# Rows gathered for a sparse expert layer: first picks in the query phase, 16 extra tokens, scores copied after all three products

## The chip, the cores and the metric

The kernel runs on one core of one Trainium2 chip. The metric is the device time of one execution, in microseconds (us). The profile is of one execution; its times count from the first instruction, and the time of that execution is a little longer than its span.

The engines are called by the profile's names: PE multiplies matrices (PEld is its weight load), DVE works on vectors, ACT applies functions and copies, POOL does vector work and issues the indexed transfers, SP issues most of the plain transfers. An engine works through its own instructions in order. A matmul on 32-bit floats shows as two records in the profile.

## The reference

One step of a decoder layer for 336 tokens: 256 prompt tokens, 64 sample tokens (8 sequences of 8) and 16 learned ones that only prepare state. A first part (a convolution branch, a state-space mixer, projections) ends in `x`. The change touches the second part, an expert layer for 320 tokens:

```python
q = (xb @ w_q).reshape(T, 8, 2, 128)              # 8 heads, 2 halves
s = einsum('thcd,hckd->thck', q, keys)            # 128 keys for each half
s1, i1 = top_k(s[:, :, 0], 16);  s2, i2 = top_k(s[:, :, 1], 16)
cand = s1[..., :, None] + s2[..., None, :]        # 256 sums a head
sc, f = top_k(cand, 16)                           # 16 picks a head, 128 a token
ids = i1[f // 16] * 128 + i2[f % 16]              # of 16384 experts
act = gelu(einsum('thkd,td->thk', U[ids], xb))
y = einsum('thk,thkd->td', softmax(sc) * act, V[ids])
```

The last step adds `y` to `x` and normalizes.

## The kernel before

**Two ways to the same sum.** For most of the 320 tokens the kernel multiplies with all 16384 experts and then zeroes what wasn't picked: the dense way, `ND` = 184 tokens. For 128 tokens (`NGAT`) and 8 extra ones (`NX`) it fetches only the picked rows of U and V, 8 KB each, by an indexed transfer.

**Dense blocks.** `u_block(b)`, for 128 blocks of 128 experts, multiplies a 512 KB block of U with the tokens `nd` (8 matmuls of 184 columns into PSUM, line 1429), and ACT writes the gelu to `S` (line 1431). `v_block(b)`, again 128 times, multiplies a 512 KB block of V with `S[b]` into the sum `va` (line 1531). Blocks come into a ring of 8 buffers (`eraw`, line 1412); even blocks are issued on SP, odd ones mostly on ACT. The first 8 blocks of U lie in buffers of their own (`pre`) and are read ahead in the query phase. Between blocks `g_step` builds, for 8 tokens at a time and each half of the experts, the weights of the picks (DVE makes one-hot tiles `oh`, PE multiplies them into `pg`, DVE multiplies `S` by that).

**Gathered rows.** A column `c` of `gid` holds, for each of the 128 tokens, the number of one picked expert. `gather(c)` fetches 128 rows of 8 KB (U and V side by side) into one of 5 buffers `wuv` (`UV`). `pick_dot` multiplies with the token (DVE, line 1317), ACT applies gelu and the softmax weight (lines 1319 and 1322), `pick_sum` adds the V half into `ygat` (DVE, line 1327), which frees the buffer. The 8 extra tokens are laid out 16 times over the partitions, so that their 128 picks take 8 columns of 128 rows; their sums go to `acce`, and `group_sum` adds them up. In all that makes `NCOL` = 136 columns.

**Pace.** `gather` makes the transfer wait for a matmul of the fifth-last block issued in the program so far (`LEAD` = 4). `ahead(n)` issues columns `n` to `n+3` (to `n+1` in the second half of the V blocks). `Feed` deals the tasks out among the blocks: `NU` = (42, 26, 35) says how many columns are paired with the U blocks up to 84, with the other U blocks, and with the first 64 V blocks; the rest follow among the last V blocks up to block 126. The U blocks up to 84 also carry the ranking of the dense tokens (`topk_tasks`) and of heads 4 to 7 of the gathered ones. Some buffers of that ranking are given up at block 84.

**Query phase.** For each of 16 halves of heads (`j`), `weight` fetches 512 KB of `w_q` and splits it into a high part `wh` (ACT) and a low part `wl` (POOL, in four pieces, line 253), `proj` does 24 matmuls (line 182), ACT copies the result to `qT`, and three products with the keys, one for each group of 128, 128 and 64 tokens, give the scores `psc` (line 1206). ACT copies each to `sco` or `sall` (line 1208), and for the gathered tokens `top16` ranks them on DVE. Inside the loop a product is followed by its copy and then by the next product into the same tile. After `j` = 7, `heads_tasks(0)` ranks the candidate sums of heads 0 to 3 and writes `gid`, and `ahead(0)` issues the first gathers.

A scheduler sets the order of each engine's instructions from the program's order, the dependencies and its own clock; the order shown below is what it gave.

Of the kernel before, what the change touches and what calls it, by code (L numbers as in the profile page):

```python
# [7 lines left out]
F32 = mybir.dt.float32  # L8
# [25 lines left out]
PH = 8  # L34
NK = 128
# [1 line left out]
NM = T - T2  # L37
SQ = T2 - NQ * TS
NGAT = 128
NX = 8  # L40
XQ = 128 // max(NX, 1)
ND = T2 - NGAT - NX
NPICK = 128
NCOL = NPICK + (NPICK // XQ if NX else 0)
XAT = 64
HG = 4
EXTRA = 5
LEAD = 4
GT = 8
# [6 lines left out]
AGAIN = 24  # L56
HB = 64
KTILES = ((0, NGAT), (128, 128), (256, 64))
NU = (42, 26, 35)
LM = (0.05, 0.05, 0.1, 0.5, 0.999)  # L60
LOW = 400
NW0 = 3
# [9 lines left out]
LATER = 8  # L72
# [92 lines left out]
def body(tc, ia, oa, stop=None):  # L165
    nc = tc.nc
    with ExitStack() as top:
# [125 lines left out]
        def misc(shape, name):  # L293
            return ps.tile(shape, F32, name=name, tag="misc", bufs=2)
# [764 lines left out]
        def top16(vals, idx, v, h, late=False):  # L1059
            L = v.shape[0]  # L1060
            i_ = nc.vector.max(vals[:L, h, 0:8], v)
            if late:
                tc.add_manual_dep(i_.ins, early[0], mybir.DependencyInfo(mybir.DependencyClass.NoSync,
                                                                         mybir.DependencyReason.DATA),
                                  reason="gathered tokens first")
            nc.vector.max_index(idx[:L, h, 0:8], vals[:L, h, 0:8], v)  # L1066
            nc.vector.match_replace(v, vals[:L, h, 0:8], v, -3.0e38)
            nc.vector.max(vals[:L, h, 8:16], v)
            nc.vector.max_index(idx[:L, h, 8:16], vals[:L, h, 8:16], v)
# [45 lines left out]

        early = []

        def heads_tasks(h0):
            hs_ = slice(h0, h0 + HG)
            cs = slice(16 * h0, 16 * (h0 + HG))  # L1120
            st = {}

            def cand():
                st["sf"] = table(128, HG, si[0][:, 2 * h0:2 * h0 + 2 * HG])
                st["c"], st["cf"] = candidates(128, HG, sv[0].rearrange("p (h c) k -> p h c k", c=2)[:, hs_])

            def pick(half):
                if half == 0:
                    st["ab"] = places(128, HG, ci0.rearrange("p h k -> p (h k)")[:, cs])
                    st["pk"] = kp.tile([128, 2, HG * 16], F32, name="pkh")  # L1130
                look(st["pk"][:, half], 128, HG, st["ab"][half], st["sf"], half, st["c"])

            def soft():
                idf = kp.tile([128, HG * 16], F32, name="idh")
                nc.vector.scalar_tensor_tensor(idf, st["pk"][:, 0], float(NK), st["pk"][:, 1], op0=OP.mult, op1=OP.add)
                early.append(nc.vector.tensor_copy(gid[:, cs], idf).ins.name)
                g_ = kp.tile([128, HG, 16], F32, name="gh")
                nc.vector.tensor_tensor(g_, cv0[:, hs_], cv0[:, hs_, 0:1].to_broadcast([128, HG, 16]), op=OP.subtract)
                if h0:
                    nc.scalar.activation(g_, g_, AF.Exp, scale=rsT[:, 0:1])  # L1140
                else:
                    act(g_, g_, AF.Exp, scale=rsT[:, 0:1])
                sm = kp.tile([128, HG], F32, name="smh")
                nc.vector.tensor_reduce(sm, g_, axis=AX.X, op=OP.add)
                nc.vector.reciprocal(sm, sm)
                nc.vector.tensor_tensor(ggw[:, cs].rearrange("p (h k) -> p h k", k=16), g_,
                                        sm[:, :, None].to_broadcast([128, HG, 16]), op=OP.mult)

            return ([(1.5, cand)] + [(1.3, lambda h=h: top16(cv0, ci0, st["cf"][:, h], h0 + h)) for h in range(HG)]
                    + [(2.5, lambda: pick(0)), (2.0, lambda: pick(1)), (1.0, soft)])  # L1150

# [41 lines left out]
        for j in range(16):  # L1193
# [6 lines left out]
            proj(p[:, :T2], w, rows(ah[:, :, :T2], al[:, :, :T2]))  # L1200
            qT = qTs[j % 3]
            nc.scalar.copy(qT[:, :T2], p[:, :T2])
            p = misc([128, 3, NK], "psc")
            for i, (t0, L) in enumerate(KTILES):
                n, up = 2 * heads_of[i], 64 * (j // (2 * heads_of[i]))
                nc.tensor.matmul(p[:, i], qT[:, t0 - up:t0 - up + 128], keys[:, j, :], start=True, stop=True)
                s_ = sall[i][:, j % n] if i else kp.tile([128, NK], F32, name="sco", bufs=9)
                scored = nc.scalar.copy(s_[up:up + L], p[up:up + L, i]).ins.name
                if i == 0:
                    top16(sv[i], si[i], s_[:L], j)  # L1210
# [4 lines left out]
            if j == EXTRA:  # L1215
                extra_tokens()
                xs.close()
            if j == 2 * HG - 1:
                for _, f_ in heads_tasks(0):
                    f_()  # L1220
            if j == 2 * HG - 1:
                ahead(0)
        xqs.close()
        parts = [(0, SA), (SA, SB), (SB, 128)]
        Sm = []
# [122 lines left out]
        def take(n):  # L1348
            t = ops[:n]
            del ops[:n]  # L1350
            return t

        def mixin(a_, b_):
# [3 lines left out]
                out += b_[q * nb // na:(q + 1) * nb // na]  # L1357
            return out

        t1, t2 = topk_tasks(1), topk_tasks(2)  # L1360
        bg = mixin(t1[:-1] + t2[:-5] + t1[-1:] + t2[-5:-1], take(NU[0] - 4 - LATER)) + take(4) + t2[-1:]
        bg += mixin(heads_tasks(HG), take(LATER))

        class Feed:
            def __init__(self, tasks, steps):
# [302 lines left out]
```

## Time and profile before

| | before |
|---|---|
| three runs | 1278.71, 1280.62, 1280.56 us |
| median | 1280.56 us |
| the profiled execution | 1278.62 us |
| its span | 1276.8 us |
| busy DVE / ACT / POOL | 961.7 / 520.4 / 595.6 us |
| moved by the DMA engines | 373.82 MB, of it 142.62 MB by the 136 gathers |
| granted TensorE clock | 0.995 on the mean |

The span falls in three parts: the layer's first part up to 520 us, the query phase up to about 600 us (its last scores reach ACT at 619 us), and the dense blocks with the gathers, up to 1266 us, with a tail of 11 us.

In a row of the timeline stand the start, the duration, the engine, the line of the kernel, the operation, the tile written and those read, the shape, and how many instructions are merged; in brackets stands how long the engine had been idle and what released it. In a row by stretches stand, for each engine, busy us and the number of instructions, then the granted clock, the share of time that the 16 DMA engines were busy, and what they moved in GB/s.

### The profile page before, as it was taken

To read this page: it belongs to the slowest core of one execution; us is meant where nothing else is said; L and a number is where in the kernel's file an instruction comes from. 1 tells how busy PE (TensorE), PEld (TensorE's weight loads), DVE (VectorE), ACT (ScalarE), POOL (GpSimd) and SP (SyncE) were. 2 spreads that over 40 slices of the span, in tenths; PEclk is the share of its full clock that TensorE was granted. 3 is DMA by queue.
4 is the path that set the end of the run, shared out by engine and by line. 5 is a ranking of instruction groups with operands and counts; after the bars stand their busy time and mean duration, and the time that the engine had idled before them with its cause. 6 is when DMAs were issued, how large, how long until landed. Compare 5 with 4: busy or idle time off the path is not lost.

```text
span 1276.8 us, 23637 instructions
## 1 busy us (share of the span) xinstructions
PE 1257.3 (98%) x8953; PEld 1214.0 (95%) x8953; DVE 961.7 (75%) x2121; ACT 520.4 (41%) x1308; POOL 595.6 (47%) x595
## 2 busy tenths in 40 slices
PE   9999999999999999999999999999999999999997
PEld 7989999999889999999999999999999999999997
DVE  6888889888977335549999978888888888545555
ACT  6778777887766444544232222222210111001102
POOL 2487777887795766975132232223322322122110
PEclk9899999999999999999999999999999999999999
DMA  6435454344434444765989999999999999999994
GB/s 248 166 130 194 158 190 169 140 175 170 145 126 149 149 150 149 255 243 210 372 321 422 421 420 420 420 420 420 420 421 420 420 421 419 397 421 420 419 421 158
DMA packets 85618, 373.82 MB, mean 293 GB/s; under 512 B 9585, under 2 KB 15089, under 8 KB 65921
## 3 DMA queue, kind: packets, MB, share of 16 engines
q1 hardware_dynamic: 48048, 166.87, 34.9%
q0 software_dynamic: 19584, 142.62, 26.9%
q10 hardware_dynamic: 17872, 62.84, 12.2%
q8 instruction: 70, 1.15, 0.4%
q14 instruction: 44, 0.35, 0.1%
HBM read 359.24 MB, written 13.05 MB: 292 GB/s over the span
## 4 chain that ended last, share of the span: by engine, by line
PE 81%; DVE 15%; DMA 2%; ACT 1%; issue 1%; POOL 1%; ACTq 0%; DVEq 0%
PE pj L182 32%; PE va L1531 25%; PE pj L1429 15%; DVE wuv L1317 2%; DVE ygat L1327 2%; PE pg L1457 2%; DVE pcv L525 1%; PE pst L182 1%; DMA wuv<-in_peer_uv_dram,gid 1%; PE po L182 1%; PE py L182 1%; PE pq L182 1%; DMA wdt<-in_w_dt_dram 1%; DVE st L718 1%; DVE si L1066 1%
## 5 line engine op out<-in xcount | busy, mean ns | idle before, releaser
L1159 POOL DMA_INDIRECT wuv<-in_peer_uv_dram,gid x136 | 166.2, 1222 | 478.3 <-PE va L1531 133.7
L253 POOL TENSOR_TENSOR wl<-wraw,wh 128x256 fp32r<-128x256 f32 (+1 forms) x202 | 289.9, 1455 | 109.5 <-ACT wh L249 64.9
L1531 PE MATMUL va<-S,eraw 128*128 128x184 f32 x2048 | 325.4, 320 | 0.0
L1531 PEld LDWEIGHTS va<-S,eraw 128*128 128x128 f32 x2048 | 318.9, 190 | 0.9 <-issue 0.9
L1429 PE MATMUL pj<-nd,eraw 128*128 128x184 f32 x1792 | 290.1, 321 | 1.8 <-DMA eraw<-in_uT_dram 1.7
L1429 PEld LDWEIGHTS pj<-nd,eraw 128*128 128x128 f32 x1792 | 278.8, 190 | 2.6 <-ACT S L1431 2.2
L182 PE MATMUL pj<-ah,wh 128*128 128x336 f32 (+1 forms) x768 | 242.6, 327 | 1.5 <-ACT xg L225 1.2
L182 PE MATMUL pj<-al,wh 128*128 128x336 f32 (+1 forms) x768 | 232.6, 316 | 0.0
L1327 DVE SCALAR_TENSOR_TENSOR ygat<-wuv,scg,ygat 128x1024 f32<-128x1024 f32 x128 | 164.0, 1281 | 73.5 <-ACT scg L1322 72.9
L1317 DVE SCALAR_TENSOR_TENSOR wuv<-wuv,x2m 128x1024 f32<-128x1024 f32 x128 | 156.2, 1221 | 56.6 <-DMA wuv<-in_peer_uv_dram,gid 54.2
L1319 ACT ACTIVATE scg<-scg 128x1 f32<-128x1 f32 x136 | 27.3, 202 | 416.6 <-DVE wuv L1317 297.8
L249 ACT CAST wh<-wraw 128x1024 fp32r<-128x1024 f32 x125 | 131.0, 1049 | 78.3 <-PE pj L182 55.7
L182 PEld LDWEIGHTS pj<-ah,wh 128*128 128x128 f32 x768 | 145.4, 190 | 7.1 <-issue 2.7
L182 PEld LDWEIGHTS pj<-al,wh 128*128 128x128 f32 x768 | 145.1, 190 | 0.7
L182 PE MATMUL pj<-ah,wl 128*128 128x336 f32 (+1 forms) x768 | 138.5, 315 | 1.9 <-POOL wl L253 1.9
L525 DVE SCALAR_TENSOR_TENSOR pcv<-ch,vec,pcv 128x320 f32<-128x320 f32 x232 | 127.6, 550 | 10.8 <-ACT pcv L523 8.1
L182 PEld LDWEIGHTS pj<-ah,wl 128*128 128x128 f32 x768 | 120.3, 189 | 3.0 <-POOL wl L253 2.9
L1431 ACT ACTIVATE S<-pj 128x184 f32<-128x184 f32 x128 | 38.6, 316 | 109.7 <-PE pj L1429 100.1
L536 DVE SCALAR_TENSOR_TENSOR pj<-mcat,vec,pj 128x360 f32<-128x360 f32 x96 | 56.5, 590 | 5.5 <-ACT pj L534 5.1
L1468 DVE SCALAR_TENSOR_TENSOR S<-pg,S 128x232 f32<-128x232 f32 (+1 forms) x92 | 34.5, 417 | 14.3 <-PE pg L1457 10.4
L1322 ACT ACTIVATE scg<-scg,ggw 128x1 f32<-128x1 f32 x136 | 39.7, 294 | 6.2 <-PE va L1531 1.8
L1429 PE MATMUL pj<-nd,pre 128*128 128x184 f32 x256 | 42.0, 319 | 0.0
(392 smaller groups left out, 1693.9 us busy)
## 6 DMA issues: line engine op xcount, KB each, us to landing
wraw<-in_w_in_dram SPq DMA_DIRECT2D x80, 512.0 KB
eraw<-in_vE_dram SPq DMA_DIRECT2D x64, 512.0 KB
eraw<-in_vE_dram ACTq DMA_DIRECT2D x64, 512.0 KB
eraw<-in_uT_dram SPq DMA_DIRECT2D x60, 512.0 KB
eraw<-in_uT_dram ACTq DMA_DIRECT2D x52, 512.0 KB
st<-in_state_dram SPq DMA_DIRECT2D x8, 1024.0 KB
out_ssm_s_dram<-st SPq DMA_DIRECT2D x8, 1024.0 KB
wraw<-in_w_mo_dram SPq DMA_DIRECT2D x16, 512.0 KB
```

Of the source, the lines that this page charges most:

```text
L182: i_ = nc.tensor.matmul(*a_, **kw)
L249: (nc.vector.tensor_copy if on_dve else nc.scalar.copy)(h, src)
L253: (nc.gpsimd if on_pool else nc.vector).tensor_tensor(l[:, q:q + m], src[:, q:q + m], h[:, q:q + m].bitcast(F32), op=OP.subtract)
L525: nc.vector.scalar_tensor_tensor(to, in_, sc, eights(acc), op0=OP.mult, op1=OP.add)
L536: nc.vector.scalar_tensor_tensor(o, cat[:, w:w + n], wv, o, op0=OP.mult, op1=OP.add)
L1159: i_ = nc.gpsimd.indirect_dma_start(out=u, out_offset=None, in_=ia["peer_uv"], in_offset=bass.IndirectOffsetOnAxis(ap=gid[:, c:c + 1], axi ...
L1317: nc.vector.scalar_tensor_tensor(u[:, :D], u[:, :D], 1.0, x2m if c < NPICK else x2e, op0=OP.mult, op1=OP.mult, accum_out=w)
L1322: nc.scalar.activation(w, w, AF.Copy, scale=ggw[:, c:c + 1])
L1327: nc.vector.scalar_tensor_tensor(a_, u[:, D:], scg[:, c:c + 1], a_, op0=OP.mult, op1=OP.add)
L1429: i_ = nc.tensor.matmul(p[:, :ND], raw[:, k, :], nd[:, k, :], start=(k == 0), stop=(k == KD - 1))
L1431: nc.scalar.activation(Sv(b), p[:, :ND], AF.Gelu)
L1531: i_ = nc.tensor.matmul(va[k // 2][:, k % 2], raw[:, k, :], Sv(b), start=(b == 0 and k % 2 == 0), stop=(b == 127), skip_group_check=True)
```

## The change

It does six things.

1. `NX` goes from 8 to 16, so `ND` from 184 to 176, `NCOL` from 136 to 144. Dense matmuls have 176 columns; there are 22 `g_step`s for each half of the experts, where there were 23; and 8 more gathers.
2. In the query phase the three products go one after the other into a tile of another PSUM tag (`y`), and the three copies come after them.
3. Heads 0 to 3 of the gathered tokens are ranked in two steps of two heads (`HB0`), after `j` = 3 and after `j` = 7.
4. `SOON` issues the gathers of columns 0 to 2 after `j` = 3 and of columns 3 and 4 after `j` = 7, where `ahead(0)` issued columns 0 to 3 after `j` = 7.
5. The first 6 column tasks (`NSOON`) come at once, ahead of the first U block's tasks; the others are dealt out by `NU` = (52, 26, 36).
6. The late rankings of the dense tokens are ordered behind the second write of `gid` (`early[1]`).

```diff
-NX = 8
+NX = 16
 HG = 4
+HB0 = 2
+SOON = {3: (0, 1, 2), 7: (3, 4)}
+NSOON = 6
-NU = (42, 26, 35)
+NU = (52, 26, 36)
...
-                tc.add_manual_dep(i_.ins, early[0], mybir.DependencyInfo(mybir.DependencyClass.NoSync,
+                tc.add_manual_dep(i_.ins, early[1], mybir.DependencyInfo(mybir.DependencyClass.NoSync,
...
-        def heads_tasks(h0):
+        def heads_tasks(h0, HG):
...
-            p = misc([128, 3, NK], "psc")
+            p = ps.tile([128, 3, NK], F32, name="psc", tag="y", bufs=2)
+            ups = [64 * (j // (2 * n)) for n in heads_of]
             for i, (t0, L) in enumerate(KTILES):
-                n, up = 2 * heads_of[i], 64 * (j // (2 * heads_of[i]))
-                nc.tensor.matmul(p[:, i], qT[:, t0 - up:t0 - up + 128], keys[:, j, :], start=True, stop=True)
+                nc.tensor.matmul(p[:, i], qT[:, t0 - ups[i]:t0 - ups[i] + 128], keys[:, j, :], start=True, stop=True)
+            for i, (t0, L) in enumerate(KTILES):
+                n, up = 2 * heads_of[i], ups[i]
...
-            if j == 2 * HG - 1:
-                for _, f_ in heads_tasks(0):
+            if j in (HG - 1, 2 * HG - 1):
+                for _, f_ in heads_tasks(j // 2 - HB0 + 1, HB0):
                     f_()
-            if j == 2 * HG - 1:
-                ahead(0)
+            if j in SOON:
+                for n in SOON[j]:
+                    pend[n] = gather(COLS[n])
...
+        for _, f_ in take(NSOON):
+            f_()
         t1, t2 = topk_tasks(1), topk_tasks(2)
-        bg = mixin(t1[:-1] + t2[:-5] + t1[-1:] + t2[-5:-1], take(NU[0] - 4 - LATER)) + take(4) + t2[-1:]
-        bg += mixin(heads_tasks(HG), take(LATER))
+        bg = mixin(t1[:-1] + t2[:-5] + t1[-1:] + t2[-5:-1], take(NU[0] - 4 - LATER - NSOON)) + take(4) + t2[-1:]
+        bg += mixin(heads_tasks(HG, PH - HG), take(LATER))
```

How this moves instructions shows in three places. The line numbers of the changed kernel are 3 higher than before up to the score products, and 5 to 8 higher behind them.

POOL, query phase before: the splits of the last weights of `w_q` (`wl`, four rows a weight), the extra tokens (`x2e`), and then all the gathers.

```order
L1024 TENSOR_TENSOR x2m<-x2m,wuv 128x1024
L253 TENSOR_TENSOR wl<-wraw,wh 128x256 x28
L1054 TENSOR_TENSOR x2e<-x2e,wuv 128x512
L253 TENSOR_TENSOR wl<-wraw,wh 128x256 x4
L1054 TENSOR_TENSOR x2e<-x2e,wuv 128x512
L253 TENSOR_TENSOR wl<-wraw,wh 128x256 x12
```

POOL, the same place in the changed kernel.

```order
L1027 TENSOR_TENSOR x2m<-x2m,wuv 128x1024
L256 TENSOR_TENSOR wl<-wraw,wh 128x256 x8
L1057 TENSOR_TENSOR x2e<-x2e,wuv 128x512
L256 TENSOR_TENSOR wl<-wraw,wh 128x256 x4
L1057 TENSOR_TENSOR x2e<-x2e,wuv 128x512
L256 TENSOR_TENSOR wl<-wraw,wh 128x256 x4
L1162 DMA wuv<-in_peer_uv_dram,gid 128x2048 x5
L256 TENSOR_TENSOR wl<-wraw,wh 128x256 x28
L1162 DMA wuv<-in_peer_uv_dram,gid 128x2048 x139
```

The first five gathers now stand between the splits of the ninth and the tenth weight; the splits of seven weights stand behind them. All five read columns of head 0, so they wait for the first of the two writes of `gid`.

DVE, the first product with a gathered row (`wuv,scg<-wuv,x2m`) before; ahead of it the whole of `gid` for heads 0 to 3 has been written, and what stands around it is the ranking of scores (`sall` of the dense tokens, `sco` of the gathered ones).

```order
L1067 MATCH_REPLACE sall_6448<-sv_6443,sall_6448 128x128
L1068 MAX sv_6442<-sall_6447 128x8
L1069 MAX_INDEX si_6445<-sv_6442,sall_6447 128x8
L1068 MAX sv_6443<-sall_6448 128x8
L1067 MATCH_REPLACE sco<-sv_6441,sco 128x128
L1068 MAX sv_6443<-sall_6448 128x8
L1317 SCALAR_TENSOR_TENSOR wuv,scg<-wuv,x2m 128x1024
```

DVE, the first such product in the changed kernel; `cv` and `ci` belong to the ranking of heads 2 and 3.

```order
L1084 TENSOR_TENSOR cand<-sv_6441 128x2x16
L1093 CAST sf<-si_6444 128x256
L1064 MAX cv_6449<-cand 128x8 x2
L1323 SCALAR_TENSOR_TENSOR wuv,scg<-wuv,x2m 128x1024
L1069 MAX_INDEX ci_6450<-cv_6449,cand 128x8 x2
L1070 MATCH_REPLACE cand<-cv_6449,cand 128x136 x2
L1064 MAX sv_6441<-sco 128x8
L1071 MAX cv_6449<-cand 128x8 x2
L1069 MAX_INDEX si_6444<-sv_6441,sco 128x8
L1072 MAX_INDEX ci_6450<-cv_6449,cand 128x8
L1323 SCALAR_TENSOR_TENSOR wuv,scg<-wuv,x2m 128x1024
```

The products with rows 0 to 4 have moved into the ranking of heads 2 and 3, ahead of the second write of `gid`.

PE, the end of the query phase before: the last score products (`psc`) stand in ones among the first U blocks (`pj<-nd`).

```order
L1429 MATMUL pj<-nd,pre 128x184 x12
L1206 MATMUL psc<-keys,qT_6452 128x128
L1206 MATMUL psc<-keys,qT_6451 128x128
L1429 MATMUL pj<-nd,pre 128x184 x10
L1206 MATMUL psc<-keys,qT_6452 128x128
L1206 MATMUL psc<-keys,qT_6451 128x128
L1429 MATMUL pj<-nd,pre 128x184 x10
L1206 MATMUL psc<-keys,qT_6452 128x128
L1206 MATMUL psc<-keys,qT_6453 128x128
L1429 MATMUL pj<-nd,pre 128x184 x8
```

PE, the same place in the changed kernel.

```order
L185 MATMUL pj<-ah,wl 128x320 x2
L1209 MATMUL psc<-keys,qT_6453 128x128 x3
L185 MATMUL pj<-ah,wl 128x320 x6
L1437 MATMUL pj<-nd,pre 128x176 x12
L1209 MATMUL psc<-keys,qT_6451 128x128 x3
L1437 MATMUL pj<-nd,pre 128x176 x44
L1437 MATMUL pj<-nd,eraw 128x176 x64
L1437 MATMUL pj<-nd,pre 128x176 x64
```

All but the last three score products now stand ahead of the run of U blocks, and the last three 12 matmuls into it.

## The prediction

> **What bounds the kernel now.** I read the table by stretches first, then PE's timeline, POOL's gathers and the end.
>
> ```profile
> core 0: us, PE busy (x) PEld busy (x) DVE busy (x) ACT busy (x) POOL busy (x), PEclk, DMA share, GB/s
> 540.00:600.00 60.00, 59.74 (x419) 58.88 (x418) 37.97 (x202) 27.40 (x69) 39.10 (x51) 1.00 0.57 201
> 600.00:620.00 20.00, 20.00 (x137) 20.00 (x136) 20.00 (x115) 5.57 (x22) 3.75 (x4) 1.00 0.99 403
> 620.00:660.00 40.00, 40.00 (x259) 40.00 (x258) 40.00 (x158) 10.41 (x34) 9.63 (x9) 1.00 0.84 315
> 660.00:1250.00 590.00, 588.23 (x4333) 581.75 (x4332) 442.85 (x795) 96.07 (x361) 151.63 (x122) 1.00 1.02 418
> 1250.00:1260.00 10.00, 10.00 (x66) 10.00 (x65) 6.28 (x13) 3.82 (x10) 0.00 (x0) 1.00 0.40 162
> ```
>
> From 660 to 1250 us PE is busy for 588.23 of 590 us, and the DMA engines are full as well (1.02, 418 GB/s). Two resources bind together, so relief of one shows what the other allows.
>
> ```profile
> 652.01 37.56 PE L1429 MATMUL pj<-nd,eraw 128*128 128x184 f32 x240
> 1206.11 60.00 PE L1531 MATMUL va<-S,eraw 128*128 128x184 f32 x384
> PE pj L1429 <- DMA eraw<-in_uT_dram: 1.7, 2, 1.2
> ```
>
> A dense matmul's record takes 60.00/384 = 0.1563 us (37.56/240 gives 0.1565). A block has 4096/256 = 16 records, so 2.50 us. The third row is PE's wait for U blocks from 600 to 1265 us: 1.7 us in two waits. So PE still sets the pace, and DMA only just keeps up.
>
> ```profile
> q0 software_dynamic: 19584, 142.62, 26.9%
> eraw<-in_vE_dram SPq DMA_DIRECT2D x64, 512.0 KB
> 1221.82 0.94 POOL L1159 DMA_INDIRECT wuv<-in_peer_uv_dram,gid  x1 [4.05 <-PE va L1531]
> 1226.81 0.94 POOL L1159 DMA_INDIRECT wuv<-in_peer_uv_dram,gid  x1 [4.05 <-PE va L1531]
> 1234.29 1.37 POOL L1159 DMA_INDIRECT wuv<-in_peer_uv_dram,gid  x1 [4.05 <-PE va L1531]
> 1253.49 1.22 DVE L1317 SCALAR_TENSOR_TENSOR wuv<-wuv,x2m 128x1024 f32<-128x1024 f32 x1 [1.85 <-DMA wuv<-in_peer_uv_dram,gid]
> ```
>
> A gather is 142.62/136 = 1.049 MB, a block 512 KB = 0.524 MB; at 418 GB/s that is 2.51 and 1.25 us. POOL's late gathers are released by PE. The last is issued at 1234.29 and its first product starts at 1253.49, 19.2 us later.
>
> ```profile
> 1261.08 2.42 DVE L1525 SCALAR_TENSOR_TENSOR wraw<-x2e,frs,wuv 128x512 f32<-128x512 f32 x2
> 1264.28 0.32 ACT L1543 ACTIVATE sqd<-va 128x184 f32<-128x184 f32 x1 [3.16 <-PE va L1531]
> 1264.64 0.41 DVE L1546 TENSOR_SCALAR nd<-va,fn 128x184 f32<-128x184 f32 x1 [1.14 <-ACT sqd L1543]
> 1272.83 1.24 ACTq L1552 DMA_DIRECT2D out_yd_dram<-nd  x2
> ```
>
> PE ends at 1206.11 + 60.00 = 1266.1; the tail to 1276.8 is 10.7 us. The gathered tokens end at 1261.08 + 2.42 = 1263.5, which is 10.0 us after the last gather's arrival and 2.6 us before PE: a second path close behind the first.
>
> **The change part by part.** The profiled execution took 1278.62 us, 1.8 more than its span, and stands 1.9 us below the median of 1280.56, so my sum sits on the low side of the runs by that.
>
> *176 columns.* In proportion a record takes 0.1563 × 176/184 = 0.1495 us, a block 2.39, and 256 blocks lose 256 × 0.109 = 28 us of PE. The bounds are no gain (0.1563) and the weight load; the nearest row for that is this one.
>
> ```profile
> 576.70 1.32 PE L182 MATMUL pj<-ah,wl 128*128 128x320 f32 x8
> 577.86 0.49 PE L1206 MATMUL psc<-keys,qT 128*128 128x128 f32 x3
> ```
>
> Eight matmuls, each with new weights, fit between 576.70 and 577.86: 0.145 each. So weights allow 0.145, and I take 0.1495. Two `g_step`s fewer for each half gain PE another 1 to 2 us. None of the 28 us counts by itself, since DMA is full.
>
> *Eight more gathers.* I sum the bytes from 600 to 1260 us: 20 × 403 + 40 × 315 + 590 × 418 + 10 × 162 (in KB) = 268.9 MB. Eight gathers add 8.39 MB. Five gathers that were issued behind 598 us come before it and take 5.24 MB out of the stretch, if they move as the order says. That leaves 272.0 MB, +3.1 MB, **+7.5 us** at 418 GB/s. Without the early five it would be +20 us.
>
> The Trainium skill speaks against leaning on 418: "DMA: Bandwidth & Descriptors", section "Where 436 GB/s comes from", says that about 358 GB/s of memory bandwidth limits transfers from HBM. The row with 418 GB/s over 590 us contradicts that for one core, and the measurement decides; at 358 the three net gathers would cost 8.8 instead of 7.5 us.
>
> *The idle stretch behind the first gathers.*
>
> ```profile
> 550.04 5.71 POOL L253 TENSOR_TENSOR wl<-wraw,wh 128x256 fp32r<-128x256 f32 x8 [0.26 <-ACT sall L1208]
> 560.40 2.82 POOL L253 TENSOR_TENSOR wl<-wraw,wh 128x256 fp32r<-128x256 f32 x4 [4.66 <-ACT sall L1208]
> 598.25 0.19 DVE L1136 CAST gid<-idh 128x64 int32<-128x64 f32 x1
> 598.73 1.14 POOL L1159 DMA_INDIRECT wuv<-in_peer_uv_dram,gid  x1 [7.54 <-DVE sv L1061]
> 603.90 0.94 POOL L1159 DMA_INDIRECT wuv<-in_peer_uv_dram,gid  x1 [0.30 <-issue]
> 626.22 1.27 DVE L1327 SCALAR_TENSOR_TENSOR ygat<-wuv,scg,ygat 128x1024 f32<-128x1024 f32 x1
> 628.25 0.94 POOL L1159 DMA_INDIRECT wuv<-in_peer_uv_dram,gid  x1 [23.41 <-DVE sv L1068]
> ```
>
> `gid` is written at 598.25, five gathers fill the five buffers by 604.84, and the sixth waits for the first sum (626.22): 23.4 us without an issue, while DVE works without a pause (20.00 of 20.00, 40.00 of 40.00). From 600 to 660 the DMA engines could have moved 60 × 418 = 25.1 MB and moved 20.7, so 4.4 MB or 10.6 us were lost.
>
> When will they come now? `gid` for heads 0 and 1 needs the scores of halves 0 to 3, the second `gid` those up to half 7.
>
> ```profile
> 536.49 0.30 DVE L1061 MAX8 sv<-sco 128x8 f32<-128x128 f32 x1 [1.02 <-ACT sco L1208]
> 556.42 0.29 DVE L1061 MAX8 sv<-sco 128x8 f32<-128x128 f32 x1 [4.28 <-ACT sco L1208]
> 578.58 0.29 DVE L1061 MAX8 sv<-sco 128x8 f32<-128x128 f32 x1 [1.11 <-ACT sco L1208]
> ```
>
> These are the first rankings of halves 0, 3 and 7 of the gathered tokens: 5 to 7 us a half, where PE needs 24 × 0.145 = 3.5. From half 7 to `gid` went 598.25 − 578.58 = 19.7 us for four heads; two heads take half, 9.9. So `gid` for heads 0 and 1 comes between 536.5 + 3 × 3.5 + 9.9 = 557 (PE's pace) and 556.4 + 9.9 = 566 (as before), the second between 571 and 588. POOL has split the ninth weight by 550.04 + 5.71 = 555.8 and then stands at the gathers. I take 557, because each half's products no longer wait for a copy between them, and 584, near the late end, because five products with rows now lie ahead of it. Five issues at the old spacing (603.90 + 0.94 − 598.73 = 6.1 us) hold POOL until 563. The stretch from 540 to 600 leaves 418 − 201 = 217 GB/s: 4.8 us a gather, so the fifth lands at about 581.
>
> From `gid` to the first sum went 28.0 us before; five products of 1.2 us less leave about 22, plus one for the order: 607 instead of 626. DMA's pause is then 19 us shorter less the time that blocks fill anyway. I take a little under half of the 10.6 us as won, **−5.1 us**; bounds 0 (sum not earlier) and −10.6 (no idle left). DMA then ends 7.5 − 5.1 = 2.4 us later, and the last gather's arrival moves from 1253.5 to about 1255.9.
>
> *What PE does with it.* PE now waits for blocks in the middle, so its reserve is eaten: before, PE finished 1266.1 − 1253.5 = 12.6 us (five blocks) behind the last arrival. From the last gather's issue PE needed 1266.1 − 1234.3 = 31.8 us, 12.7 blocks; now 12.75 × 2.39 = 30.5 us. DMA had 15.7 × 418 + 10 × 162 = 8.2 MB left then; I add 1.8 MB, three and a half of the five blocks of reserve, since a buffer or two stay filled: 10.0 MB, 23.9 us. So PE ends 30.5 − 23.9 = 6.6 us behind DMA: 1262.5, **−3.6 us**. Bounds: 2.4 us (last block only, −7.8) and 12.6 us (nothing eaten, +2.4).
>
> *The tail* works on 176 columns in place of 184: in proportion 0.4 of its 10.7 us, of which I take −0.3.
>
> *DVE.*
>
> ```profile
> L1317 DVE SCALAR_TENSOR_TENSOR wuv<-wuv,x2m 128x1024 f32<-128x1024 f32 x128 | 156.2, 1221 | 56.6 <-DMA wuv<-in_peer_uv_dram,gid 54.2
> L1327 DVE SCALAR_TENSOR_TENSOR ygat<-wuv,scg,ygat 128x1024 f32<-128x1024 f32 x128 | 164.0, 1281 | 73.5 <-ACT scg L1322 72.9
> ```
>
> Eight columns more are 8 × (1.221 + 1.281) = 20 us, hidden: DVE has 590 − 442.85 = 147 us free. Uncovered, in the end alone, a column costs 2.5. Ranking in twos doubles some 20 small instructions of 0.19 to 0.22 us (lines 1135 and 1136 among them): 4 us, where DVE is busy for 37.97 of 60. I take 0; bounds 0 and +4.
>
> *Scores as three products, then copies.*
>
> ```profile
> L1206 PE MATMUL psc<-keys,qT x96: 270/275/377, 534.1 to 618.9; 128*128 128x128 f32 x96
>   DVE sv L1061: 23.4, 10
> ```
>
> The instructions stay the same; DVE's 23.4 us of waiting for scores (ten times) goes in part, and it is this that brings `gid` forward. PE, 59.74 of 60 us busy ahead of 600, has nothing to win there. What is left is bounded by −2 and +3 (one half's pace either way); taken 0. The order behind `early[1]` only moves rankings of dense tokens behind the products, taken 0 within the same bounds.
>
> Sum: 1276.8 − 3.6 − 0.3 = 1272.9 span, **1274.6 us** with 1.8 around it.
>
> **The rivals.**
>
> *Gathers come last (no change).* The y path is 10.0 us behind the last arrival. If DMA's last transfer is a gather (arrival 1255.9), y ends at 1265.9, and the dense tail's DVE work queues behind it: 1265.9 + 10.5 = 1276.4, 1278.2 us. For it: 2.6 us of slack only. Against: the blocks behind the last gather come through the same queues.
>
> The trace has a gather each 4.99 us (1221.82 to 1226.81) beside two blocks of 2.50 us, equal bytes, so a gather has about half of the bandwidth. The Trainium skill ("DMA: Bandwidth & Descriptors", section "Queues, rings and completion order") has the engines take turns between the queues; by that, with two block queues, a gather would get a third, 7.5 us, the last ones would come later and this rival be likelier. The measured half decides.
>
> *The early gathers stall POOL (slower).* They stand ahead of the splits of weights 10 to 16. If `gid` of heads 0 and 1 is late, POOL waits, `wl` comes late and PE's query products with it, and the five gathers are not moved into the idle stretch: 5.24 MB or 12.5 us return. 1272.9 + 12.5 = 1285.4, **1287 us**. It decides from `gid` later than about 564: the tenth split started at 560.40 after 4.66 us of idle, and five issues of 6.1 us come between. For it: my late end, 566, lies beyond that point, and a wait there holds 28 splits. Against: DVE is 37% free, and blocks can fill PE for a while.
>
> *PE's saving is real (much faster).* If transfers did not bind, 1276.8 − 28 = 1249, 1251 us. Against it stand 590 us at a DMA share of 1.02.
>
> **How the numbers follow.** Forecast 0.55, own range 1268 to 1278 (the bounds −7.8 and +2.4 on PE's end, with the 5.1 uncertain both ways); gathers last 0.22; POOL stalls 0.18; full saving 0.05. About 0.2% (2.6 us) is what a measurement can tell from no change. The range is 1266 to 1287: it takes in the stall and leaves the full saving out. Forecast and full saving give 0.60 faster; gathers last 0.22 same; the stall 0.18 slower.
>
> **What would show it.** Right: the first five gathers on POOL at 556 to 564; first `ygat` sum near 607; records of 0.149 us; waits of PE for `eraw` of 15 us and more; a DMA share near 1.0 from about 610; the last gather's product at 1251 to 1257; PE's end near 1262. Wrong: splits starting after 565 behind a wait on `gid` (stall); the y path ending after PE (gathers last); PE without waits and a span near 1250 (full saving); or gathers that lose their place to the blocks, so that the first sum is later than 615.

## The result, and the profile after

| | before | after |
|---|---|---|
| median of the runs | 1280.28 us (4 runs) | 1295.84 us (4 runs) |
| ratio | | 1.0125, 95% interval 1.0107 to 1.0142 |
| the profiled execution, its span | 1278.62, 1276.8 us | 1297.57, 1295.8 us |
| PE's last `va` matmul ends | 1266.1 | 1285.2 |
| product with the last gathered rows | 1253.5 | 1269.8 |
| bytes moved, by gathers | 373.82, 142.62 MB | 382.15, 151.00 MB |

The changed kernel is slower by about 15 us (1.25%), where 6 us less was predicted, and outside the range. The span grew by 19.0 us, PE's end by 19.1; the tail behind it is 10.6 us (before 10.7).

The table by stretches of the changed kernel, with the columns of the one shown of before:

```profile
540.00:600.00 60.00, 55.66 (x389) 55.16 (x389) 57.79 (x215) 26.13 (x69) 48.05 (x56) 0.97 0.70 258
600.00:620.00 20.00, 20.00 (x138) 20.00 (x137) 20.00 (x138) 5.67 (x21) 0.00 (x0) 1.00 0.71 229
620.00:660.00 40.00, 35.91 (x234) 34.58 (x233) 40.00 (x136) 9.05 (x28) 12.16 (x11) 1.00 0.95 364
660.00:1250.00 590.00, 568.04 (x4228) 554.51 (x4227) 445.62 (x787) 94.50 (x372) 152.53 (x128) 0.99 1.01 416
```

From 660 us on PE is no longer always busy (568 of 590 us, before 588), and the DMA engines are as full as before (416 GB/s). Most of PE's saving has become waiting. Ahead of that, the stretch from 600 to 620 moves 229 GB/s where it moved 403, with no instruction on POOL.

PE's timeline at the end, and from DVE's the product with the last gathered rows:

```profile
1226.75 48.10 PE L1539 MATMUL va<-S,eraw 128*128 128x176 f32 x320
1275.43 9.81 PE L1539 MATMUL va<-S,eraw 128*128 128x176 f32 x64 [0.58 <-DMA eraw<-in_vE_dram]
1269.82 1.23 DVE L1323 SCALAR_TENSOR_TENSOR wuv<-wuv,x2m 128x1024 f32<-128x1024 f32 x1 [1.88 <-DMA wuv<-in_peer_uv_dram,gid]
```

Two rows of PE's waits from 600 us on (us in total, times, the longest):

```profile
PE va L1539 <- DMA eraw<-in_vE_dram: 8.0, 9, 3.9
PE pj L1437 <- DMA eraw<-in_uT_dram: 6.6, 5, 3.1
```

A record takes 48.10/320 = 0.1503 us, as forecast. But PE now waits 14.6 us for blocks, to the last four, and still needs 9.8 us from their arrival. Another 11.7 us of its waits are for ACT and DVE.

POOL and DVE around the first gathers, both from their timelines, in order of time:

```profile
563.19 0.17 DVE L1139 CAST gid<-idh 128x32 int32<-128x32 f32 x1
563.64 1.14 POOL L1162 DMA_INDIRECT wuv<-in_peer_uv_dram,gid  x1 [4.89 <-DVE sv L1071]
569.94 21.19 POOL L256 TENSOR_TENSOR wl<-wraw,wh 128x256 fp32r<-128x256 f32 x24
597.20 0.17 DVE L1139 CAST gid<-idh 128x32 int32<-128x32 f32 x1
620.26 1.26 DVE L1333 SCALAR_TENSOR_TENSOR ygat<-wuv,scg,ygat 128x1024 f32<-128x1024 f32 x1
621.80 0.95 POOL L1162 DMA_INDIRECT wuv<-in_peer_uv_dram,gid  x1 [27.12 <-DVE sv L1071]
```

The first gather comes 35 us earlier than before (563.64 against 598.73), but the first sum only 6 us earlier (620.26 against 626.22), and the second write of `gid` only 1 us. So five buffers are filled by 582 us or so and stay full until 620; the sixth gather is issued at 621.80. The stretch without an issue grew from 23.4 to some 52 us (569.9 to 621.8). The early gathers moved bytes forward, and by 620 us DMA had moved as many fewer.

Summed from the trace's packets, the bytes moved by a time show it in one table (MB; the last three columns are the runs e7, e9 and e5, told of below).

| by | before | after | score copies alone | score copies and 16 tokens | (52, 26, 36) alone |
|---|---|---|---|---|---|
| 600 us | 103.5 | 106.8 | 105.7 | 105.1 | 103.4 |
| 620 us | 111.5 | 111.4 | 114.0 | 113.4 | 111.1 |
| 640 us | 118.4 | 118.1 | 122.4 | 121.8 | 118.2 |
| 1250 us | 370.9 | 371.6 | 372.5 | 374.0 | 367.3 |
| in all | 373.9 | 382.2 | 373.9 | 382.2 | 373.9 |

After 620 us before and after run on the same curve; the changed kernel has 8.3 MB more to go, 20 us at 418 GB/s.

### The profile page after: what moved, and what is told of

Read it like the earlier page. It is cut to its first block, busy times and chain, and to the rows that moved or that the text cites. A ratio compares the mean times of both kernels' runs of the same rounds, so it can differ in the third digit from the quotient of the medians.

```text
span 1295.8 us, 23650 instructions
## 1 busy us (share of the span) xinstructions
PE 1247.2 (96%) x8921; PEld 1195.4 (92%) x8921; DVE 995.2 (77%) x2159; ACT 518.9 (40%) x1325; POOL 604.8 (47%) x603
## 2 busy tenths in 40 slices
DMA packets 86802, 382.15 MB, mean 295 GB/s; under 512 B 9728, under 2 KB 15232, under 8 KB 66080
## 3 DMA queue, kind: packets, MB, share of 16 engines
q0 software_dynamic: 20736, 151.00, 28.1%
## 4 chain that ended last, share of the span: by engine, by line
PE 52%; DMA 25%; DVE 18%; issue 2%; ACT 1%; POOL 1%; ACTq 0%; DVEq 0%; POOLq 0%
PE pj L185 30%; DMA wuv<-in_peer_uv_dram,gid 19%; PE va L1539 11%; DMA eraw<-in_vE_dram 4%; PE pj L1437 3%; DVE ygat L1333 3%; DVE wuv L1323 3%; DVE pcv L528 1%; PE pst L185 1%; PE po L185 1%; PE py L185 1%; DMA eraw<-in_uT_dram 1%; PE pg L1465 1%; POOL wl L256 1%; PE pq L185 1%
## 5 line engine op out<-in xcount | busy, mean ns | idle before, releaser
L1162 POOL DMA_INDIRECT wuv<-in_peer_uv_dram,gid x144 | 170.7, 1185 | 500.5 <-PE va L1539 105.6
L256 POOL TENSOR_TENSOR wl<-wraw,wh 128x256 fp32r<-128x256 f32 (+1 forms) x202 | 294.6, 1477 | 97.2 <-ACT wh L252 65.1
L1539 PE MATMUL va<-S,eraw 128*128 128x176 f32 x2048 | 318.0, 316 | 8.0 <-DMA eraw<-in_vE_dram 8.0
L1539 PEld LDWEIGHTS va<-S,eraw 128*128 128x128 f32 x2048 | 307.3, 191 | 14.0 <-DMA eraw<-in_vE_dram 13.1
L1437 PE MATMUL pj<-nd,eraw 128*128 128x176 f32 x1792 | 285.4, 319 | 9.9 <-DMA eraw<-in_uT_dram 6.6
L1437 PEld LDWEIGHTS pj<-nd,eraw 128*128 128x128 f32 x1792 | 272.7, 193 | 13.4 <-ACT S L1439 6.8
L1323 DVE SCALAR_TENSOR_TENSOR wuv<-wuv,x2m 128x1024 f32<-128x1024 f32 x128 | 159.2, 1244 | 99.5 <-DMA wuv<-in_peer_uv_dram,gid 99.1
L528 DVE SCALAR_TENSOR_TENSOR pcv<-ch,vec,pcv 128x320 f32<-128x320 f32 x232 | 128.4, 553 | 10.7 <-ACT pcv L526 8.0
L1439 ACT ACTIVATE S<-pj 128x176 f32<-128x176 f32 x128 | 36.1, 306 | 36.3 <-PE pj L1437 34.9
L1437 PE MATMUL pj<-nd,pre 128*128 128x176 f32 x256 | 41.5, 319 | 1.6 <-ACT S L1439 1.6
L1437 PEld LDWEIGHTS pj<-nd,pre 128*128 128x128 f32 x256 | 39.5, 194 | 2.4 <-ACT S L1439 2.4
## 6 DMA issues: line engine op xcount, KB each, us to landing
eraw<-in_uT_dram ACTq DMA_DIRECT2D x52, 512.0 KB, 10.7
```

What stands on the lines that cost most here:

```text
L256: (nc.gpsimd if on_pool else nc.vector).tensor_tensor(l[:, q:q + m], src[:, q:q + m], h[:, q:q + m].bitcast(F32), op=OP.subtract)
L528: nc.vector.scalar_tensor_tensor(to, in_, sc, eights(acc), op0=OP.mult, op1=OP.add)
L1162: i_ = nc.gpsimd.indirect_dma_start(out=u, out_offset=None, in_=ia["peer_uv"], in_offset=bass.IndirectOffsetOnAxis(ap=gid[:, c:c + 1], axi ...
L1323: nc.vector.scalar_tensor_tensor(u[:, :D], u[:, :D], 1.0, x2m if c < NPICK else x2e, op0=OP.mult, op1=OP.mult, accum_out=w)
L1437: i_ = nc.tensor.matmul(p[:, :ND], raw[:, k, :], nd[:, k, :], start=(k == 0), stop=(k == KD - 1))
L1439: nc.scalar.activation(Sv(b), p[:, :ND], AF.Gelu)
```

## The experiments

Theory A: DMA's bytes set the end, and the eight gathers cost 8 × 2.5 us. Theory B: POOL's wait for the early row numbers makes the query phase, and PE for good, late. Later came C (the dealing out), D and P: D is that the new score copies make the query phase late, P that DVE and POOL hold each other up ("the port"). Times are medians, with the median of before that was measured beside them in brackets; spans are those of the profiled executions, before 1276.8. "Query phase" stands for all of the change but its width and the numbers `NU`, "score copies" for its part 2, "twos" for the ranking in twos with the order behind `early[1]`, and "port eased" for a wait put into POOL's splits.

| run | tokens extra | what else | time (before) | span |
|---|---|---|---|---|
| the change | 16 | all | 1295.8 (1280.3) | 1295.8 |
| e1 | 8 | all | 1305.0 (1278.9) | 1303.6 |
| e2 | 16 | dealing out | 1298.1 (1278.9) | 1297.8 |
| e3 | 16 | all, 136 gathers | 1289.2 (1278.9) | 1286.3 |
| e4 | 16 | all, sums early | 1293.3 (1278.9) | 1292.1 |
| e5 | 8 | dealing out | 1295.7 (1279.5) | 1294.2 |
| e6 | 8 | query phase | 1291.3 (1279.5) | 1292.8 |
| e7 | 8 | score copies | 1276.0 (1279.5) | 1272.8 |
| e8 | 32 | all | 1343.1 (1279.5) | 1340.5 |
| e9 | 16 | score copies | 1292.5 (1279.4) | 1290.9 |
| e10 | 8 | score copies, twos | 1284.0 (1279.4) | 1283.0 |
| e11 | 8 | query phase, port eased | 1288.6 (1279.4) | 1288.2 |
| e12 | 16 | query phase | 1300.3 (1279.4) | 1298.0 |
| e13 | 8 | as e10, port eased | 1280.1 (1279.0) | 1280.3 |
| e14 | 8 | query phase, port eased | 1289.8 (1279.0) | 1289.7 |

### e1: the change without its width

```diff
-NX = 16
+NX = 8
```

> The whole change but its width: 8 extra tokens, 184 dense columns and 136 gathers as before, with the new score copies, ranking in twos, early gathers and dealing out. Theory A (bytes): the loss is 8 gathers x 2.5 us = 20 us on a full DMA, the other edits move nothing, so 1277 to 1283 us, same as before. Theory B (order): POOL's wait for the row numbers and the late query phase put PE 6 to 8 us behind for good, so 1287 us or more.

1305.0 us, ratio 1.0205 (95% interval 1.0188 to 1.0222): the width undone makes it slower still. Theory A for the whole falls: at 184 columns the other edits cost 26 us. PE reaches U block 8 at 622.6 (before 611.0) and block 80 at 826.0 (before 798.9), and from there the distance stays at 27 us to the end: PE is the limit at this width and gets nothing back. In the query phase it waits once for 6.9 us, a wait that the changed kernel doesn't have (told of with e10).

### e2: the width and the dealing out alone

```diff
-NX = 8
+NX = 16
-NU = (42, 26, 35)
+NU = (52, 26, 36)
```

> Only the width and the dealing out on the kernel before: 16 extra tokens, 176 dense columns, 144 gathers, columns dealt out by (52, 26, 36); scores, ranking and first gathers as before. Theory A (bytes): 1280 + 20 = about 1298 us less what the reserve gives, 1294 to 1300 us, same as the changed kernel. Theory B (order): 1283 to 1289 us, since POOL's wait and the late query phase are gone.

1298.1 us, ratio 1.0151 (1.0134 to 1.0168), as A said. At 176 columns the query phase of the change costs nothing beside this (1295.8 with it). So what a part costs depends on which of PE and DMA is the limit, though not on that alone: the wait of 6.9 us stands only in runs at 184 columns that rank in twos.

### e3: eight gathers fewer at 176 columns

```diff
-                    pend[i_] = gather(COLS[i_])
+                    pend[i_] = pend[i_ - 1] if COLS[i_] >= NPICK and COLS[i_] % 2 else gather(COLS[i_])
```

> The changed kernel with 136 gathers in place of 144: eight of the 16 extra columns work on the rows of the column ahead (their sums are wrong by that), all else the same, products and sums too. Theory A (bytes): 8 x 2.5 = 20 us off 1295.8, so 1274 to 1279 us. Theory B (order): within 4 us of the changed kernel, 1291 us or more.

The kernel leaves out eight transfers; the columns they were for work on the rows of the column ahead, so its sums differ.

1289.2 us: 6.6 less than the change, between the two. The table by stretches of this run shows why:

```profile
900.00:950.00 50.00, 44.53 (x336) 43.89 (x335) 48.60 (x77) 11.91 (x47) 6.00 (x6) 0.93 0.86 328
950.00:1250.00 300.00, 300.00 (x2251) 293.95 (x2250) 198.16 (x309) 31.39 (x124) 66.97 (x62) 1.00 1.02 419
```

Where the gathers are left out DMA falls to 328 GB/s, 92 below its 420 (92 GB/s × 50 us = 4.6 MB, 11 us), PE stands 5.5 us for a one-hot tile of DVE, and behind it PE is busy for 300 of 300 us: it is the limit there, late by what it lost earlier.

### e4: the first sums early

```diff
...
+            if j == 2 * HG - 1:
+                for n in range(5):
+                    pick_dot(n, False)
+                for n in range(5):
+                    pick_sum(n)
...
```

The rest of the edit moves the two functions up and takes these five columns out of the later loop.

> The changed kernel with the products and sums of columns 0 to 4 written directly behind the ranking of heads 2 and 3 in the query loop, so that the sums no longer stand behind the last score copies and the dense rankings. Theory A (bytes, with the pause of DMA at 590 to 622 us as what is left to win): first sum before 595 us, over 380 GB/s from 600 to 620, and 5 to 10 us less: 1286 to 1291 us. Theory B (order): splits behind waiting gathers hold the query phase further, 1296 us or more.

1293.3 us, 2.5 less, where 5 to 10 were expected. The first sum came at 572.5, but DMA moved 364 GB/s from 600 to 620, not over 380, and PE reached block 8 at 622.5 (616.6 in the change). DMA was 3.8 MB ahead of the change at 620 us (115.2 against 111.4) but only 1.4 MB at 1250; PE waited 11.0 us for one-hot tiles (`oh`) of DVE in between, and DMA moved 411 GB/s from 800 to 900. The direction is A's, the size isn't.

### e5: the dealing out alone

```diff
-NU = (42, 26, 35)
+NU = (52, 26, 36)
```

> The kernel before (136 gathers, 184 columns, its own query phase) with nothing but the dealing out changed: (52, 26, 36) in place of (42, 26, 35), so ten more columns among the first 84 U blocks. Theory A (bytes alone): the same bytes on a full DMA, 1277 to 1282 us. Theory C (dealing): the first U blocks then have more bytes than DMA can move in their PE time (10 x 2.5 us), PE waits there, and as PE is the limit behind, it doesn't get that back: 1286 to 1296 us.

1295.7 us, ratio 1.0137 (1.0116 to 1.0158), in theory C's range. Ten more columns among the first 84 U blocks, with not a byte more in all, cost the kernel before 16 us. PE reaches block 8 as before (611.1) and block 80 at 814.5 (before 798.9). Its stretch from 700 to 800 us:

```profile
700.00:800.00 100.00, 88.30 (x593) 86.81 (x592) 81.62 (x175) 20.86 (x79) 24.03 (x21) 0.95 1.02 421
```

PE's waits in that run:

```profile
PE pg L1457 <- DVE oh L1453: 4.7, 1, 4.7
PE pj L1429 <- DMA eraw<-in_uT_dram: 3.6, 2, 2.9
PE pxi L1303 <- DVE S L1468: 3.2, 1, 3.2
```

PE stands for 11.7 of 100 us, for blocks only in part (2.9 us there), and for 7.9 us for DVE, which has the rows to wait for ahead of its one-hot tiles. Theory C had all of it as waits for blocks. DMA is full there and 3.5 MB short at 1250 us: behind, PE needs fewer bytes than DMA could move (361 GB/s from 1200 to 1250).

### e6 and e7: the query phase, and its score copies alone

```diff
 # e6: the change with
-NX = 16
+NX = 8
-NU = (52, 26, 36)
+NU = (42, 26, 35)
```

> The whole change but its width and its dealing out: 136 gathers, 184 columns, dealt out by (42, 26, 35), with the new score copies, ranking in twos and early gathers. Theory C (dealing is most of the 26 us of the run with the width of before): 1284 to 1290 us, with PE at block 8 still some 10 us late. Theory D (the query phase is most of it): 1298 us or more. Theory A: 1277 to 1282 us.

e7 is the kernel before with part 2 of the change and nothing else:

> The kernel before with only the score products in one tile and the copies behind them. Theory D (query phase, from this edit): PE loses the U blocks that filled the query phase and starts block 8 later, 1284 to 1290 us. Theory B (query phase, from POOL's wait for the early row numbers): no change here, 1276 to 1282 us.

e6 took 1291.3 us (1.0095, 1.0078 to 1.0112), near C's range and 10.9 us late at block 8. e7 took 1276.0 us (0.9978, 0.9968 to 0.9988), **faster** than before, by 3.5 us, at the lower end of B's range, though neither theory had a gain: D falls. DVE and POOL of that run, from their timelines:

```profile
581.94 0.17 DVE L1136 CAST gid<-idh 128x64 int32<-128x64 f32 x1
582.40 1.14 POOL L1159 DMA_INDIRECT wuv<-in_peer_uv_dram,gid  x1 [1.46 <-DVE sv L1061]
604.59 1.25 DVE L1329 SCALAR_TENSOR_TENSOR ygat<-wuv,scg,ygat 128x1024 f32<-128x1024 f32 x1
606.61 0.95 POOL L1159 DMA_INDIRECT wuv<-in_peer_uv_dram,gid  x1 [15.27 <-DVE sco L1067]
```

And its row by stretches:

```profile
600.00:640.00 40.00, 40.00 (x259) 40.00 (x257) 40.00 (x168) 9.02 (x29) 10.16 (x8) 1.00 1.02 420
```

`gid` for all four heads is written at 581.94 instead of 598.25, the first sum comes at 604.59 instead of 626.22, and DMA is full from 600 to 640 (420 GB/s). ACT's last score copies come at 596.6 instead of 619.2, and the gelu of the first row stands behind them. No early gathers are needed for it, and PE waits for no block.

### e8: 32 extra tokens

```diff
-NX = 16
+NX = 32
-NU = (52, 26, 36)
+NU = (58, 29, 40)
```

> The changed kernel with 32 extra tokens: 160 gathers, 160 dense columns, dealt out by (58, 29, 40). Theory A (bytes): 16 more gathers x 2.5 us = 40 us on top of 1295.8, 1331 to 1338 us. A theory in which PE's lateness sets the time gives less, since PE has 16 columns less: under 1315 us.

1343.1 us, 47 more than the change and 5 above A's range. The page has 398.80 MB, 16.65 more, at 414 GB/s from 660 to 1250: 40.2 us. Sixteen gathers cost their bytes and 5 to 7 us beside them, although PE has 16 columns less. The end isn't PE's here:

```profile
PE prd L1552 <- ACT sqd L1551: 28.2, 2, 27.8
```

PE is done with its blocks at 1300.5 us and stands 27.8 us, while the last gathers are issued 3.03 us apart (1304.63 to 1307.66), each behind the sum that frees its buffer, and DMA moves 215 GB/s from 1300 to 1330. The gathers come last, which the sum over bytes leaves out.

### e9 and e12: 16 extra tokens with other dealing

e9 is e7 with `NX = 16` and `NU = (46, 28, 38)`; e12 is the change with `NU = (42, 26, 35)`.

> The kernel before with the new score copies and 16 extra tokens: 144 gathers, 176 columns, dealt out by (46, 28, 38); ranking, first gathers and their order as before. Theory A (the end is where the bytes end): 382.2 MB in all, 122.4 MB of them moved by 640 us with the new score copies, the rest at 420 GB/s ends at 1255 to 1258, PE 10 us later, tail 10.6: 1277 to 1283 us. A theory in which the 20 us of the width come whatever else is done: 1294 us or more.

> The changed kernel (144 gathers, 176 columns) dealt out by (42, 26, 35) as before. Theory A (at this width DMA is full whatever the dealing): 1293 to 1298 us, as the changed kernel. Theory C (dealing costs 16 us at any width): 1280 to 1284 us.

e9 took 1292.5 us, ten above what A gave; PE's end is at 1280.0. It has the lead of e7 nearly whole (121.8 MB by 640 us), and 374.0 MB by 1250, 8.2 short of all: DMA made 413 GB/s from 640 to 1250 (382 from 660 to 700), where I had counted on 420, and PE waited 16.9 us for blocks. The kernel before made 414 over that stretch and the changed one 416, so 420 was too much to count on. From e7 the width costs 18.1 us of span. e12 took 1300.3 us, a little above A's range and far from C's: at this width the old dealing wins nothing. Its end is a different one, first a row of PE's waits:

```profile
PE prd L1552 <- ACT sqd L1551: 12.4, 2, 12.1
```

and from the timelines of PE and DVE:

```profile
1265.85 7.43 PE L1539 MATMUL va<-S,eraw 128*128 128x176 f32 x48 [1.36 <-DMA eraw<-in_vE_dram]
1275.92 1.22 DVE L1323 SCALAR_TENSOR_TENSOR wuv<-wuv,x2m 128x1024 f32<-128x1024 f32 x1
```

PE is done at 1273.3, the last product with gathered rows starts at 1275.92, and the dense tail waits 12 us behind the gathered tokens: the rival that gathers come last, in another kernel.

### e10, e11, e13, e14: ranking in twos, early gathers, and DVE's port

The trace of e6 shows where its query phase stands still. DVE, POOL, ACT and PE, each from its timeline:

```profile
543.84 11.38 DVE L1086 TENSOR_TENSOR cand<-sv 128x240 f32<-128x240 f32 x1
544.81 4.89 POOL L256 TENSOR_TENSOR wl<-wraw,wh 128x256 fp32r<-128x256 f32 x7
553.56 1.40 POOL L256 TENSOR_TENSOR wl<-wraw,wh 128x256 fp32r<-128x256 f32 x2
559.77 0.32 ACT L228 ACTIVATE gh<-gh,rsT 128x32 f32<-128x32 f32 x1 [9.92 <-DVE gh L1141]
560.00 0.41 ACT L1205 COPY qT<-pj 128x320 f32<-128x320 f32 x1
560.46 1.65 PE L1209 MATMUL psc<-keys,qT 128*128 128x128 f32 x6 [6.86 <-ACT qT L1205]
```

DVE's addition of the candidates of heads 0 and 1 takes 11.38 us here and ends 0.3 us behind an unbroken run of POOL (to 554.96). Behind it ACT's exp of the scores stands for 9.92 us, behind that in ACT's order the copy of `qT`, and PE waits 6.86 us. The same addition in the changed kernel:

```profile
544.29 0.41 DVE L1086 TENSOR_TENSOR cand<-sv 128x240 f32<-128x240 f32 x1
```

There it takes 0.41 us, under a run of POOL that is unbroken as well (542.06 to 558.75), and PE has no wait for `qT`. It takes 0.40 to 0.41 us in e3, e4 and e12 too, and 11.38 us in e1, e6 and e10, with 6.9 us of PE each time. So this wait is no part of what the change cost; it is a cost of the runs at 184 columns. e10 keeps the score copies and the ranking in twos, issues columns 0 to 3 after `j` = 7 as before (`SOON` = {7: (0, 1, 2, 3)}, `NSOON` = 0) and lets these four gathers wait for the second `gid`; e11 and e14 put one wait into e6, e13 into e10 (shortened):

```diff
 # e10, e13: in gather, for the first four
+                tc.add_manual_dep(i_.ins, early[1], Sync, "rows later")
 # e11 (j == 6), e13 and e14 (j == 5): first piece of that weight's split
+                tc.add_manual_dep(i_.ins, cands[0], Sync, "behind the candidates")
```

> Width and dealing out as before (136 gathers, 184 columns, (42, 26, 35)), new score copies, ranking in twos; but the first four gathers wait for the second write of the row numbers, so none stands early on POOL. Theory B (POOL's wait for the early row numbers is the loss of the query phase): 1275 to 1279 us, as with the score copies alone. Theory P (DVE's ranking in twos falls under POOL's run of splits, and DVE waits for the port that they share): PE still late at block 8, 1284 us or more.

> The run with the query phase alone (1291.3 us), and POOL's split of the seventh weight waits for DVE's addition of the candidates of heads 0 and 1, which took 11.4 us in that run while POOL split without a pause. Theory P: the addition takes under 3 us, PE's wait of 6.9 us for qT goes, block 8 comes 5 to 9 us earlier, 1282 to 1287 us. Theory B: within 3 us of 1291.

> The run with ranking in twos and no early gathers (1284.0 us), and POOL's split of the sixth weight waits for DVE's addition of the candidates of heads 0 and 1, so that the addition comes ahead of POOL's run. Theory P (the 8 us that ranking in twos costs beside the score copies alone are the port): the addition takes under 1 us, PE's wait of 6.9 us goes, 1275 to 1279 us. Otherwise 1282 to 1285 us.

> The same wait of the sixth split in the run with the early gathers (1291.3 us, 136 gathers, 184 columns). Theory P alone: 1279 us or less. Theory P and B together (the early gathers cost their part still): 1283 to 1287 us, with the DMA engines below 300 GB/s from 600 to 620 us.

The addition in e11 and in e13:

```profile
544.00 5.43 DVE L1094 TENSOR_TENSOR cand<-sv 128x240 f32<-128x240 f32 x1
```

```profile
544.14 2.65 DVE L1094 TENSOR_TENSOR cand<-sv 128x240 f32<-128x240 f32 x1
575.57 0.32 ACT L1152 ACTIVATE gh<-gh,rsT 128x32 f32<-128x32 f32 x1 [6.49 <-DVE gh L1150]
576.25 1.65 PE L1222 MATMUL psc<-keys,qT 128*128 128x128 f32 x6 [3.77 <-ACT qT L1218]
```

e10 took 1284.0 us: ranking in twos (with the order behind `early[1]`) costs 8 us beside the score copies alone (1276.0), with no gather early, so B isn't all. Where POOL pauses earlier, the addition ends earlier: 11.38, 5.43, 2.65 us, though not within the 3 and 1 us that theory P gave. PE reaches block 8 earlier by it, at 617.3 instead of 621.9 (e11 against e6) and at 618.0 instead of 620.7 (e13 against e10). The medians fall from 1291.3 to 1288.6, 1.6 us above P's range, and from 1284.0 to 1280.1, 1 us above it; but the intervals overlap (e6 1.0078 to 1.0112, e11 1.0042 to 1.0083; e10 1.0009 to 1.0042, e13 0.9992 to 1.0016), so it is the traces that show the gain. In e13 the second exp holds ACT and PE once more (6.49 and 3.77 us), with no long instruction of DVE ahead. e14 took 1289.8, above its range of 1283 to 1287: the early gathers, with the first six column tasks that come with them, cost another 10 us beside e13; PE waits 4.6 us once for a split, and DMA moves 230 GB/s from 600 to 620.

## Why the prediction was wrong

**What bounds the kernel** was read rightly: two resources, both full. After, e2, and e8 up to 1300 us, show DMA as the limit at 176 columns and fewer, e1, e5 and e6 show PE at 184.

**176 columns.** 0.1503 us a record against 0.1495 forecast; the 28 us of PE are real, and most of them became waits.

**Eight more gathers.** The price of 2.5 us each holds: 8.33 MB more, 20 us. The step that failed is the subtraction, "Five gathers … come before it and take 5.24 MB out of the stretch". At 600 us the changed kernel was 3.3 MB ahead, at 620 us 0.1 MB behind. A gather that is issued earlier takes a byte out of the stretch only if something else fills its place, and the buffers were full until the first sum. e4 shows that freeing them is not enough either: with the first sum at 572.5, of a lead of 3.8 MB at 620 us 1.4 MB were left at 1250, and 2.5 us were won.

**The idle stretch.** "so **−5.1 us**" measured 0: the first sum came at 620.3, not 607, and the second `gid` at 597.2, not 584. A first sum later than 615 had been named as a sign of being wrong. What the sums wait for was missed. ACT's timeline of the changed kernel:

```profile
603.88 0.56 ACT L1213 COPY sall<-psc 128x128 f32<-128x128 f32 x2
604.46 0.57 ACT L1325 ACTIVATE scg<-scg 128x1 f32<-128x1 f32 x5
```

The gelu of all five rows stands behind the last score copy, as the kernel orders it, and DVE then had rankings of scores (`sall` and `sco`) in front until 620. The ranking of heads 2 and 3 lay under 21 us of POOL's splits. One small instruction of DVE shows that:

```profile
584.92 6.25 DVE L1117 TENSOR_TENSOR pkh<-cand 128x32 f32<-128x32 bf16 x1
```

The same instruction took 0.17 us at 559.26. These two steps are 12.5 + 5.1 of the forecast; with both at 0, DMA's end moves by 2.4 + 17.6 = 20.0 us; the last product moved by 16.3, PE's end by 19.1.

**PE's reserve.** I had PE end 6.6 us behind the last gather; it was 15.4 (before 12.6). What I called a reserve to be eaten isn't one: the last four blocks arrive together at the end, and PE does them one after the other (9.8 us). Forecast −3.6, measured +19.1: of the 22.7 between them 13.9 come from the arrival (1269.8 against 1255.9), 8.8 from this.

**DVE, score copies, tail.** 20 us more of DVE were hidden. The score copies, taken at 0 with −2 as bound, are worth −4.0 us of span alone (e7), by the earlier `gid` and sum; the mechanism was named, its place wasn't: they do without early gathers what I gave to those. Ranking in twos was taken at 0 to +4 and costs 8 us at 184 columns (e10 against e7), but with the addition's wait, which the changed kernel doesn't have; with that wait shortened some 4 us are left (e13 against e7), and no run gives its size at 176 columns. The dealing out had no term of its own and costs 16 us at 184 columns (e5); at 176 the old numbers are 4.5 us slower than the new ones (e12).

**The rivals.** The early gathers did stand on POOL: the first `gid` came at 563.2, within 1 us of the point named (564), and POOL waited 4.9 us; its next split started at 569.9, later than the 565 named as the sign of a stall, and PE waited 4.3 us for one. That rival's price was right in kind (the five gathers win nothing), but its time, 1287, still had the 5.1 and the reserve in it. With both steps at 0 and the reserve as before, the forecast's own sum is 1274.6 + 12.5 + 5.1 + 6.0 = 1298.2, and 1297.57 was measured in the profiled execution. That this is so close is partly luck: the last product moved by 16.3 us, not by 20.0, and PE ended 15.4 us behind it, not 12.6. *Gathers last* did not come, but its argument against, that the blocks come through the same queues, isn't so: in the profile the gathers go through q0 and the blocks through q1 and q10, and in e8 and e12 the gathers do come last.

**How it adds up** (spans): before 1276.8; score copies −4.0 (e7); 16 tokens with a dealing of their own +18.1 (e9); ranking in twos, early gathers and the rest of the dealing +4.9; 1295.8. These parts don't add at 184 columns, where the last group alone is worth +30.8 (e1 against e7): there PE is the limit, and each of its waits stays, the 6.9 us for `qT` among them. No version with 16 tokens was faster than before; the score copies alone beat both kernels.

## What to carry to other kernels

Where two engines are both full, a saving on one is worth what the other leaves, and a transfer that is added costs its bytes in full; compare the bytes moved by a given time, not shares. An earlier issue helps only if what frees its buffer comes earlier too, so follow the buffer to its release (here through an in-order ACT queue to the last score copy) before counting it. Try the parts alone: the small one that looked like nothing was the only gain here. And look for a wait in the trace of the kernel that is to be explained: the longest wait of the query phase in e6 isn't there in the changed kernel.

## What the runs showed of the hardware that was not expected

A DVE instruction that reads two tensors from SBUF can wait for a whole run of POOL instructions, not for one of them. In e6 the addition stood through 15 back-to-back instructions of POOL, 11.38 us, and ended when the run did; with a pause in POOL's run 5.43 and 2.65 us. It need not: in the changed kernel it passed in 0.41 us. There it had started 0.11 us ahead of POOL's next instruction, in e1, e6 and e10 0.25 to 0.27 us ahead; why that decides is not shown. In the changed kernel a 0.17 us instruction stood for 6.25 us, to the end of POOL's run at 591.13, while other small ones that read two tensors took 0.4 to 0.9 us under the same run. The Trainium skill ("SBUF — State Buffer", section "Who interferes with whom") has such an instruction of DVE contend with an instruction of GpSimd (POOL) that reads SBUF, one blocking the other fully for that instruction; the traces agree that they block, and show that POOL's next instruction can go first again.
